# State-space steps over both row halves, with 64-column output tiles and scans of four segments

## The chip, the cores and the metric

The kernel runs on one core of a Trainium2 chip, in one launch. TensorE (PE) multiplies; VectorE (DVE), ScalarE (ACT) and GpSimd (POOL) work on SBUF and PSUM beside it; SyncE (SP) issues the loads. The metric is the device time in microseconds of one execution, median of several runs.

## The reference, cut to what matters

Two residual layers on 256 tokens of 2048 channels, then an RMSNorm. The even layer is the one that the change touches:

```python
proj = rmsnorm(x) @ w_in                     # xa, ga, (u, v), gb: 1024 channels each
a  = exp(lam * dt)                           # complex, 64 groups x 64 states
h[t] = a * h[t-1] + (f * b) @ xa[t]          # per group of 16 channels
y[t] = Re(c @ h[t]) + d_skip * xa[t]
ya = gelu(y);  ya = ya * sigmoid(ya @ w_glu + b_glu) * silu(ga)
yb = gelu(u) * (w_causal @ layernorm(gelu(v)) + b_sp) * silu(gb)
x  = x + concat(ya, yb) @ w_out
```

The odd layer is differential attention with its own projections; the change leaves it alone.

## The kernel before

All large products are made exact to fp32 from float32r operands: a weight is split into a rounded half (wh) and the rest (wl), an activation likewise, and three products are summed. The weights come as a stream of 140 chunks of 1 MB, in the order v, xa, u, gb, ga (w_in, 8 chunks each), eo (the rows of w_out for yb, 8), glu (4), ep (the rows of w_out for ya, 8), then 64 chunks of layer 1's projections and 16 of its output. fetch (line 139) loads a chunk on SP into one of three buffers wr. split (line 156) makes, for each half chunk, wh on ACT (a copy, line 82) and wl on DVE (a subtraction, line 61); wh and wl have three buffers each, so the copy of a half chunk waits until PE has done with the third half before it. gemm_t (line 201) runs 24 matmuls of 512 columns a chunk, gemm_c (line 213) 48 of 256. The results stand in PSUM tiles of tag "m", two of them: v, xa, u, gb and ga have two each, so ga0 takes the place of gb0.

Beside this stream runs side work, written as generators that run_side advances. Of the state-space mixer these are: ssm_params (decays, phases, powers pw of a unit rotation), ssm_consts (line 478: the masked matrices bbr from b, cA and cN from c, and pk, products of both that are added into intra), ssm_bT (line 513: transposes of bbr into bT), e_tables (line 529: E, the rotations of 128 steps, by doubling; one for each half of the channels) and ssm_set (line 558), eight of it. Tokens go in pairs: two inputs enter one step of 128, and two outputs leave it, one by cA and one by cN.

A set S stands for one half of the channels, one of two qh and one half q of the 128 input rows, and covers four channel tiles ct. W (PSUM, one buffer) is 8 matmuls of 64 rows (line 568). On DVE: f, two products of 1024 with E and a sum and difference of 512 that turn W into the rotating frame; eight tensor_tensor_scans of 128 (line 584), each with one decay r2 broadcast along the steps; b, two products back; hst, a sum and a difference, one column to the right of the state before. y (line 594) is four matmuls with intra (line 598) and 16 with cA and cN, tiles of 32 columns, two column groups by turns (line 606). After both q, ACT makes the gelu of y into yaf.

xs (line 679 and after) is xa times the norm's factor, in its token pairs U2 on ACT, 8 copies. After u comes the spatial gate (s, line 700), into ut. After gb, ACT makes gt = silu(gb) in a tile of tag t2, which has three buffers (line 54), DVE multiplies it into ut, and PE transposes ut (ybT, line 722); after ga, at (t2 as well) and its silu.

SP's order is the order of the code. The order on the other engines is made by a scheduler from the code and its priorities; work under hp() goes ahead of what is ready beside it. A tile of a tag takes the buffer that the tile of that tag three (or two, or one) before it in the code had, and its first writer waits for the last reader of that.

Of the kernel before, what the change touches and what calls it, by code (L numbers as in the profile page):

```python
# [10 lines left out]
F32 = mybir.dt.float32  # L11
# [6 lines left out]
T = 256  # L18
# [11 lines left out]
def hybrid_trunk_kernel(ctx: ExitStack, tc: tile.TileContext, xT, xtok, w_in0, w_glu, w_out0,  # L30
# [53 lines left out]
    def rsqrt_mean(name, ss, n, eps, post=None):  # L84
        """(ss / n + eps) ** -0.5: an integer first guess, a cubic step and a Newton step."""
# [32 lines left out]
    # ---------------------------------------------------------------- weight stream  # L118
# [37 lines left out]
    def split(upto, before=None):  # L156
        """hi = the weight rounded to float32r, lo = the exact rest."""
# [80 lines left out]
    # ---------------------------------------------------------------- start: x^T, norm  # L238
# [51 lines left out]
    # the norm's factor: per token on partitions, and as a row on every partition  # L290
# [31 lines left out]
    # ---------------------------------------------------------------- SSM constants  # L322
# [34 lines left out]
    cst = {}  # L357

    def ssm_params():
# [8 lines left out]
        mul(r2, mag, mag)  # L368
# [26 lines left out]
        ep = p32("ep", 64).rearrange("p (c m) -> p c m", c=2)  # L395
# [31 lines left out]
        cst.update(ab=ab, fc=fc, fa=fa, ep=ep)  # L427
        yield
        # powers of exp(i * 2 phi): 1, 2, 4, ..., 64
        pw = []  # L430
        prev = ep
# [31 lines left out]
    def ssm_consts():  # L463
# [34 lines left out]
        # K0 = Re(C bb) and the skip, as one matrix per two pairs  # L498
        intra = cst["intra"]
        pk0 = side1("pk0", [128, 16, 32])  # L500
        for i in range(16):
            for q in range(2):
                P = i * 2 + q
                o = pk0[q * 64:q * 64 + 32, i, :]
                PE.matmul(o, bbr[0][:, P, 1, :], cN[:, 0, P, :], start=True, stop=False)
                PE.matmul(o, bbr[1][:, P, 1, :], cN[:, 1, P, :], start=False, stop=True)
        for q in range(2):
            r = slice(q * 64, q * 64 + 32)
            o = intra[r, :, q * 64:q * 64 + 32]
            add(o, pk0[r], o)  # L510
        yield
# [17 lines left out]
    def e_tables(half):  # L529
# [7 lines left out]
        for k in range(1, 7):  # L537
            n = 1 << k
            for q in range(2):
                ph = slice(q * 8, q * 8 + 8)  # L540
                es = E[:, :, ph, 0:n]
                sh = [128, 8, n]
                m = [t4(f"em{half}{k}{q}{i}", [128, 2, 8, 64])[:, :, :, 0:n] for i in range(2)]
# [12 lines left out]
    hst = sm.tile([128, 2, 4, 129], F32, name="hst", tag="hst")  # L556
    G.memset(hst[:, :, :, 0:1], 0.0)

    def ssm_set(S):
        half, q4 = S // 4, S % 4  # L560
        qh, q = q4 // 2, q4 % 2
        E = etab[half]
        er, ei = (e.rearrange("p (h c q) t -> p h q c t", h=2, q=2)[:, qh, q] for e in (E[:, 0], E[:, 1]))
# [16 lines left out]
        r2 = cst["r2"]  # L580
# [8 lines left out]
        mul(m1, g, erb)  # L589
        mul(m2, g, eib)  # L590
# [4 lines left out]
        if q == 0:  # L595
            ya["y"] = side1(f"y{S}", [128, 4, 128], 1)
            for ct in range(4):
                PE.matmul(ya["y"][:, ct, :], cst["intra"][:, (half * 2 + qh) * 4 + ct, :],
                          U2[:, half, qh, ct, :], start=ct == 0, stop=False, skip_group_check=True)
        y = ya["y"]  # L600
        for ct in range(4):
            P = (half * 2 + qh) * 8 + ct * 2 + q
# [26 lines left out]
    # ---------------------------------------------------------------- layer 0: v, spatial gate  # L629
# [40 lines left out]
    # ---------------------------------------------------------------- layer 0: xa  # L670
# [16 lines left out]
    # ---------------------------------------------------------------- layer 0: u, gb, ga  # L687
# [50 lines left out]
    # ---------------------------------------------------------------- layer 0: output projection  # L738
# [86 lines left out]
    # ---------------------------------------------------------------- layer 1  # L825
# [10 lines left out]
    # lambda  # L836
# [15 lines left out]
    def rope_evac(o, ps, name):  # L852
        """o = the rotated, normalised channels; a map's pairs lie on rows 0-15 and 32-47"""
# [95 lines left out]
            # the second query block meets all keys: its operands in two exact parts  # L949
# [175 lines left out]
```

## Time and profile before

| | us |
|---|---|
| median of 3 runs | 889.18 |
| runs, lowest to highest | 888.95 to 889.61 |
| span of the profiled execution | 887.3 |
| PE busy | 871.7 |
| DVE busy | 666.3 |
| ACT busy | 448.8 |
| PE starts u, gb, ga, eo, glu at | 103.4, 172.9, 223.7, 288.7, 335.0 |

The span runs from the first to the last instruction of the profiled execution; 1.9 us separate it from the median. Busy times overlap. A timeline row of several instructions (x8) gives the first start and the time to the last end; where a row's next start comes before its end, the distance of starts is the slot that the engine gave it.

### The profile page before, as it was taken

To read this page: it belongs to the slowest core of one execution; us is meant where nothing else is said; L and a number is where in the kernel's file an instruction comes from. 1 tells how busy PE (TensorE), PEld (TensorE's weight loads), DVE (VectorE), ACT (ScalarE), POOL (GpSimd) and SP (SyncE) were. 2 spreads that over 40 slices of the span, in tenths; PEclk is the share of its full clock that TensorE was granted. 3 is DMA by queue.
4 is the path that set the end of the run, shared out by engine and by line. 5 is a ranking of instruction groups with operands and counts; after the bars stand their busy time and mean duration, and the time that the engine had idled before them with its cause. 6 is when DMAs were issued, how large, how long until landed. Compare 5 with 4: busy or idle time off the path is not lost.

```text
span 887.3 us, 14016 instructions
## 1 busy us (share of the span) xinstructions
PE 871.7 (98%) x5598; PEld 778.4 (88%) x5598; DVE 666.3 (75%) x1219; ACT 448.8 (51%) x623; POOL 38.3 (4%) x47
## 2 busy tenths in 40 slices
PE   9999999999999999999999999999999999999995
PEld 7799978788999789889988999889988998888895
DVE  8999869999988866567866677666767577665773
ACT  6563862455334645565345543554346544554551
POOL 7110000000000100000000000000000000000000
PEclk9999999999999999999999999999999999999998
DMA  8965452234534655455554545554454455555542
GB/s 306 379 243 191 143 190 96 96 120 166 190 114 141 259 185 176 170 195 202 180 182 160 188 145 190 191 190 152 181 190 171 165 188 196 183 189 190 178 155 96
DMA packets 25985, 160.24 MB, mean 181 GB/s; under 512 B 2880, under 2 KB 4160, under 8 KB 7744
## 3 DMA queue, kind: packets, MB, share of 16 engines
q1 hardware_dynamic: 25344, 156.20, 49.2%
q0 software_dynamic: 576, 3.15, 1.0%
q8 instruction: 44, 0.72, 0.3%
q14 instruction: 21, 0.17, 0.1%
HBM read 157.24 MB, written 2.10 MB: 180 GB/s over the span
## 4 chain that ended last, share of the span: by engine, by line
PE 90%; DVE 7%; ACT 1%; issue 1%; DMA 0%; DVEq 0%; ACTq 0%
PE v L209 5%; PE v L210 5%; PE v L208 5%; PE k L224 3%; PE q L221 3%; PE k L223 3%; PE k L221 3%; PE q L224 3%; PE q L223 3%; PE g L210 3%; PE g L209 3%; PE g L208 3%; PE od L209 2%; PE od L208 2%; PE od L210 2%; PE ga L221 2%
## 5 line engine op out<-in xcount | busy, mean ns | idle before, releaser
L82 ACT ACTIVATE wh<-wr 128x1024 fp32r<-128x1024 f32 (+1 forms) x276 | 288.7, 1047 | 356.0 <-PE v L210 64.0
L61 DVE TENSOR_TENSOR wl<-wr,wh 128x1024 fp32r<-128x1024 f32 (+1 forms) x276 | 331.8, 1205 | 142.2 <-ACT wh L82 141.4
L224 PE MATMUL k<-h2h,wl 128*128 128x256 f32 x256 | 72.8, 284 | 0.0
L221 PE MATMUL q<-h2h,wh 128*128 128x256 f32 x256 | 72.7, 284 | 0.0
L223 PE MATMUL q<-h2l,wh 128*128 128x256 f32 x256 | 72.7, 284 | 0.0
L224 PE MATMUL q<-h2h,wl 128*128 128x256 f32 x256 | 72.6, 284 | 0.0
L221 PE MATMUL k<-h2h,wh 128*128 128x256 f32 x256 | 72.4, 283 | 0.0
L223 PE MATMUL k<-h2l,wh 128*128 128x256 f32 x256 | 72.4, 283 | 0.0
L209 PE MATMUL v<-wl,h2h 128*128 128x512 f32 x128 | 50.8, 397 | 0.0
L209 PE MATMUL g<-wl,h2h 128*128 128x512 f32 x128 | 50.3, 393 | 0.0
L210 PE MATMUL g<-wh,h2l 128*128 128x512 f32 x128 | 50.1, 391 | 0.0
L210 PE MATMUL v<-wh,h2l 128*128 128x512 f32 x128 | 50.0, 390 | 0.0
L208 PE MATMUL v<-wh,h2h 128*128 128x512 f32 x128 | 50.0, 390 | 0.0
L208 PE MATMUL g<-wh,h2h 128*128 128x512 f32 x128 | 49.9, 390 | 0.0
L224 PEld LDWEIGHTS k<-h2h,wl 128*128 128x128 f32 x256 | 49.1, 192 | 0.1
L221 PEld LDWEIGHTS q<-h2h,wh 128*128 128x128 f32 x256 | 49.1, 192 | 0.2
L221 PEld LDWEIGHTS k<-h2h,wh 128*128 128x128 f32 x256 | 49.1, 192 | 0.0
L223 PEld LDWEIGHTS k<-h2l,wh 128*128 128x128 f32 x256 | 49.1, 192 | 0.0
L223 PEld LDWEIGHTS q<-h2l,wh 128*128 128x128 f32 x256 | 49.1, 192 | 0.0
L224 PEld LDWEIGHTS q<-h2h,wl 128*128 128x128 f32 x256 | 49.1, 192 | 0.0
L209 PE MATMUL od<-wl,oh 128*128 128x512 f32 x96 | 37.6, 392 | 0.0
L208 PE MATMUL od<-wh,oh 128*128 128x512 f32 x96 | 37.5, 391 | 0.0
(331 smaller groups left out, 2182.8 us busy)
## 6 DMA issues: line engine op xcount, KB each, us to landing
wr<-in_w_in_dram SPq DMA_DIRECT2D x100, 1024.0 KB, 4.8
wr<-in_w_out_dram SPq DMA_DIRECT2D x32, 1024.0 KB, 4.8
wr<-in_w_glu_dram SPq DMA_DIRECT2D x4, 1024.0 KB, 4.7
wr<-in_w_in_dram SPq DMA_DIRECT2D x8, 256.0 KB, 4.5
wr<-in_w_in_dram SPq DMA_DIRECT2D x4, 512.0 KB, 7.9
xk<-in_xtok_dram SPq DMA_DIRECT2D x2, 1024.0 KB, 10.9
xr<-in_xtok_dram POOLq DMA_DIRECT2D x2, 1024.0 KB, 7.6
out_dram<-x SPq DMA_DIRECT2D x6, 256.0 KB, 2.6
```

The source lines that it names most:

```text
L61: (eng or V).tensor_tensor(out=o, in0=a, in1=b, op=op)
L82: A.activation(out=o, in_=i, func=f, **kw)
L208: PE.matmul(ps[:, t, :], hi[:, s], wh, start=first and a == 0, stop=False)
L209: PE.matmul(ps[:, t, :], hi[:, s], wl, start=False, stop=False)
L210: PE.matmul(ps[:, t, :], lo[:, s], wh, start=False, stop=last and a == len(ktiles) - 1)
L221: PE.matmul(ps[:, c, :], wh[:, s], hi, start=first and a == 0 and c % 2 == 0, stop=False, skip_group_check=True)
L223: PE.matmul(ps[:, c, :], wh[:, s], lo, start=False, stop=False, skip_group_check=True)
L224: PE.matmul(ps[:, c, :], wl[:, s], hi, start=False, stop=fin, skip_group_check=True)
```

## The change

A set S now covers both row halves q and two channel tiles a. W has a place for each q in a bank of its own, and its 8 matmuls go by turns to rows 0 to 63 and 64 to 127. The eight scans become two of 512, over four segments of 128 in a row; a tile R holds the decay of each segment with a zero at each segment's first column, which cuts the carry. R is a t2 tile: POOL clears column 0, ACT copies the broadcast r2 into the rest. hst loses its extra column and is written shifted. y is made per set: two matmuls with intra and eight with cc, 64-column tiles that hold Ca and Ca^2 side by side, both times from the same columns of hst; the second output of a step now takes its own input's and its fellow's share from intra. For that ssm_params makes a2 = a^2, ssm_consts a fourth set of masked products, and pk 128 matmuls (64 of 32 and 64 of 64 columns) where it had 64, in two halves. yaf takes 32 smaller gelus for 16. The E table's doubling works on 2 x w x n elements at once, 28 operations a half for 72, on the same elements; pw and r2 are kept in the order of the steps.

```diff
 # ssm_consts
+                ("ab", c_re, c_im, cc[0][:, :, 0, :], cc[1][:, :, 0, :], -1.0),
+                ("a2", c_re, c_im, cc[0][:, :, 1, :], cc[1][:, :, 1, :], -1.0)):
...
+            for w in range(2):
+                for i in range(8):
+                    for q in range(2):
+                        lhs = [z[:, P].rearrange("p j h -> p (j h)") if w else z[:, P, 1, :] for z in bbr]
+                        o = pk0[q * 64:q * 64 + (64 if w else 32), i, w, :]
+                        PE.matmul(o, lhs[0], cN[:, 0, P, :], start=True, stop=False, skip_group_check=True)
+                        PE.matmul(o, lhs[1], cN[:, 1, P, :], start=False, stop=True, skip_group_check=True)
 # e_tables
-                for i in range(2):
-                    a = pw[k][:, i, half * 16 + q * 8:half * 16 + q * 8 + 8].unsqueeze(2).to_broadcast(sh)
-                    for c in range(2):
-                        mul(m[i][:, c], es[:, c], a)
+                for i in range(2):
+                    a = pw[k][:, i, half * 16 + ph.start:half * 16 + ph.stop]
+                    mul(m[i], es, a.unsqueeze(1).unsqueeze(3).to_broadcast([128, 2, w, n]))
 # ssm_set
-        rows = slice(q * 64, q * 64 + 64)
-        W = side2(f"W{S}", [128, 2, 4, 128])
+        W = side2(f"W{S}", [128, 2, 2, 2, 128])
         for c in range(2):
-            for ct in range(4):
-                PE.matmul(W[:, c, ct, :], cst["bT"][c][rows, (half * 2 + qh) * 4 + ct, :],
-                          U2[rows, half, qh, ct, :], start=True, stop=True)
+            for a in range(2):
+                for q in range(2):
+                    rows = slice(q * 64, q * 64 + 64)
+                    ct = cp * 2 + a
+                    PE.matmul(W[:, q, c, a, :], cst["bT"][c][rows, (half * 2 + qh) * 4 + ct, :],
+                              U2[rows, half, qh, ct, :], start=True, stop=True)
+        R = t2(f"R{S}", [128, 4, 128])
+        G.memset(R[:, :, 0:1], 0.0)
+        act(R[:, :, 1:128], cst["r2"][:, P:P + 4].unsqueeze(2).to_broadcast([128, 4, 127]), AF.Copy)
...
-            for ct in range(4):
-                P = (half * 2 + qh) * 8 + ct * 2 + q
-                V.tensor_tensor_scan(out=g[:, c, ct, :], data0=r2[:, P:P + 1].to_broadcast([128, 128]),
-                                     data1=g[:, c, ct, :], initial=0.0, op0=ALU.mult, op1=ALU.add)
+            gf = g[:, c].rearrange("p s t -> p (s t)")
+            V.tensor_tensor_scan(out=gf, data0=R.rearrange("p s t -> p (s t)"), data1=gf, initial=0.0,
+                                 op0=ALU.mult, op1=ALU.add)
...
-        sub(h[:, 0, :, 1:129], m1[:, 0], m2[:, 1])
-        add(h[:, 1, :, 1:129], m1[:, 1], m2[:, 0])
+        sub(h[:, 0, :, 1:128], m1[:, 0, :, 0:127], m2[:, 1, :, 0:127])
+        add(h[:, 1, :, 1:128], m1[:, 1, :, 0:127], m2[:, 0, :, 0:127])
...
-            for i, cm in ((0, cst["cA"]), (1, cst["cN"])):
-                o = y[q * 64 + i * 32:q * 64 + i * 32 + 32, ct, :]
-                for c in range(2):
-                    PE.matmul(o, cm[:, c, P, :], h[:, c, ct, i:i + 128], start=False, stop=c == 1,
-                              skip_group_check=True)
+        for a in range(2):
+            for c in range(2):
+                for q in range(2):
+                    PE.matmul(y[q * 64:q * 64 + 64, a, :], cst["cc"][c][:, P + a * 2 + q].rearrange("p i h -> p (i h)"),
+                              h[:, c, q * 2 + a, :], start=False, stop=c == 1, skip_group_check=True)
```

How this moves the instructions at the end of gb. On ACT, before, around the first silu of gb (gt00, gt01 are those of gb0; wh28 to wh30 are copies of chunks of gb):

```order
L82 ACTIVATE wh28_0_2439<-wr28_2369 128x1024
L82 ACTIVATE yaf_1372<-y2_1406 32x512 x4
L82 ACTIVATE wh28_1_2443<-wr28_2369 128x1024
L82 ACT_TABLE_LOAD
L82 ACTIVATE gt00_2471<-gb0_2334,rs0_187 128x512
L82 ACTIVATE wh29_0_2494<-wr29_2403 128x1024
L82 ACTIVATE gt01_2474<-gb0_2334,rs0_187 128x512
L82 ACTIVATE wh29_1_2498<-wr29_2403 128x1024
L82 ACTIVATE wh30_0_2528<-wr30_2437 128x1024
```

and after (R7 is the decay row of set 7, y4 the output of set 4, wh32 and wh33 copies of chunks of ga):

```order
L82 ACTIVATE wh33_0_2568<-wr33_2476 128x1024
L82 ACTIVATE R7_1901<-r2_278 128x4x127
L82 ACTIVATE yaf_1352<-y4_1795 32x256 x4
L82 ACT_TABLE_LOAD
L82 ACTIVATE gt00_2387<-gb0_2250,rs0_187 128x512
L82 ACTIVATE gt01_2390<-gb0_2250,rs0_187 128x512
L82 ACTIVATE gt10_2544<-gb1_2407,rs0_187 128x512
L82 ACTIVATE gt11_2547<-gb1_2407,rs0_187 128x512
L82 ACTIVATE yh1_2248<-ybT0_2393 128x512
L82 ACT_TABLE_LOAD
```

The silus of gb0 stood among the copies of gb's own chunks; now all four stand in a row behind R7 and the gelu of y4.

On PE, before, at the last half chunk of gb (gb1) and the first matmuls of ga0:

```order
L208 MATMUL gb1_2491<-wh31_1_2566,hh1_153 128x512
L221 MATMUL ga0_2649<-hh0_152,wh32_0_2596 128x256
L223 MATMUL ga0_2649<-hl0_154,wh32_0_2596 128x256
L209 MATMUL gb1_2491<-wl31_1_2567,hh1_153 128x512
L210 MATMUL gb1_2491<-wh31_1_2566,hl1_155 128x512
L208 MATMUL gb1_2491<-wh31_1_2566,hh1_153 128x512
```

and after:

```order
L210 MATMUL gb1_2407<-wh31_1_2482,hl1_155 128x512
L600 MATMUL W5_1810<-U2_208,bT0_1022 128x128 x4
L600 MATMUL W5_1810<-U2_208,bT1_1023 128x128 x4
L637 MATMUL y4_1795<-hst_209,cc0_603 64x128 x2
L637 MATMUL y4_1795<-hst_209,cc1_604 64x128 x2
L637 MATMUL y4_1795<-hst_209,cc0_603 64x128 x2
L637 MATMUL y4_1795<-hst_209,cc1_604 64x128 x2
L600 MATMUL W6_1851<-U2_208,bT0_1022 128x128 x4
L600 MATMUL W6_1851<-U2_208,bT1_1023 128x128 x4
L632 MATMUL y5_1836<-U2_208,intra_582 128x128 x2
L753 MATMUL ybT0_2393<-ident_132,ut_1933 128x128
L637 MATMUL y5_1836<-hst_209,cc0_603 64x128 x2
L221 MATMUL ga0_2565<-hh0_152,wh32_0_2512 128x256
L223 MATMUL ga0_2565<-hl0_154,wh32_0_2512 128x256
```

ga0 followed gb1 directly, even ahead of its last matmuls; now W5, the products of y4, W6 and the beginnings of y5 and ybT0 stand between.

On DVE, before, at the product of ut with gt00:

```order
L61 TENSOR_TENSOR em1410_1779<-E1_1719,pw4_382 128x8x16 x2
L61 TENSOR_TENSOR ut_2017<-ut_2017,gt00_2471 128x512
L61 TENSOR_TENSOR E1_1719<-em1400_1771,em1401_1772 128x8x16 x2
L61 TENSOR_TENSOR wl29_0_2495<-wr29_2403,wh29_0_2494 128x1024
L61 TENSOR_TENSOR ut_2017<-ut_2017,gt01_2474 128x512
L61 TENSOR_TENSOR em1411_1780<-E1_1719,pw4_382 128x8x16 x2
```

and after:

```order
L61 TENSOR_TENSOR wl33_0_2569<-wr33_2476,wh33_0_2568 128x1024
L61 TENSOR_TENSOR b14_1789<-f14_1781,E1_1723 128x1024
L61 TENSOR_TENSOR b24_1790<-f14_1781,E1_1723 128x1024
L61 TENSOR_TENSOR hst_209<-b14_1789,b24_1790 128x4x127 x2
L61 TENSOR_TENSOR f15_1822<-W5_1810,E1_1723 128x1024
L61 TENSOR_TENSOR f25_1823<-W5_1810,E1_1723 128x1024
L61 TENSOR_TENSOR f15_1822<-f15_1822,f25_1823 128x512 x2
L618 SCALAR_TENSOR_TENSOR f15_1822<-R5_1819,f15_1822 128x512 x2
L61 TENSOR_TENSOR b15_1830<-f15_1822,E1_1723 128x1024
L61 TENSOR_TENSOR b25_1831<-f15_1822,E1_1723 128x1024
L61 TENSOR_TENSOR ut_1933<-ut_1933,gt00_2387 128x512
L61 TENSOR_TENSOR hst_209<-b15_1830,b25_1831 128x4x127 x2
L61 TENSOR_TENSOR f16_1863<-W6_1851,E1_1723 128x1024
```

That product stood within the building of E1, ahead of set 4; now it stands in set 5, between b and hst.

## Rows read from the trace of the kernel before

**Rows 1.** The page: busy time, share of the span and instructions of each engine; the granted clock of PE in tenths of full speed, in 40 slices; the chain that ended last, by engine.

```profile
PE 871.7 (98%) x5598; PEld 778.4 (88%) x5598; DVE 666.3 (75%) x1219; ACT 448.8 (51%) x623; POOL 38.3 (4%) x47
...
PEclk9999999999999999999999999999999999999998
...
PE 90%; DVE 7%; ACT 1%; issue 1%; DMA 0%; DVEq 0%; ACTq 0%
```

**Rows 2.** The table by stage: stretch, its length, busy time of PE, PEld, DVE, ACT and POOL (instructions), granted clock, DMA share, GB/s.

```profile
0.00:133.00 133.00, 128.61 (x869) 113.20 (x870) 116.45 (x342) 84.88 (x116) 24.54 (x28) 1.00 0.67 242
133.00:226.60 93.60, 91.73 (x553) 76.39 (x553) 89.34 (x181) 40.90 (x49) 0.00 (x0) 1.00 0.35 124
226.60:288.70 62.10, 62.10 (x543) 59.10 (x543) 55.89 (x77) 24.89 (x28) 0.00 (x0) 1.00 0.41 144
288.70:335.00 46.30, 45.94 (x226) 37.54 (x225) 33.09 (x35) 26.93 (x31) 4.10 (x7) 1.00 0.58 216
335.00:887.00 552.00, 543.30 (x3415) 492.20 (x3413) 371.58 (x585) 271.22 (x399) 9.68 (x12) 0.99 0.50 176
```

**Rows 3.** PE's timeline, the rows of u and gb with an idle time: start, us, what, and in brackets the idle time before and its releaser.

```profile
113.06 0.50 PE L209 MATMUL u<-wl,hh 128*128 128x512 f32 x1 [0.77 <-DVE wl L61]
...
131.26 0.66 PE L521 MATMUL pbt<-ident,bbr 128*128 128x128 f32 x4 [0.76 <-ACT bT L82]
...
134.94 0.50 PE L208 MATMUL u<-wh,hh 128*128 128x512 f32 x1 [0.46 <-ACT ut L82]
...
172.94 0.50 PE L208 MATMUL gb<-wh,hh 128*128 128x512 f32 x1 [1.41 <-ACT ut L82]
```

**Rows 4.** PE's timeline at the change from gb to ga, and the first rows of eo and glu.

```profile
223.23 0.39 PE L210 MATMUL gb<-wh,hl 128*128 128x512 f32 x1
223.45 0.39 PE L208 MATMUL gb<-wh,hh 128*128 128x512 f32 x1
223.68 0.28 PE L221 MATMUL ga<-hh,wh 128*128 128x256 f32 x1
...
226.43 0.28 PE L224 MATMUL ga<-hh,wl 128*128 128x256 f32 x1
226.55 0.28 PE L221 MATMUL ga<-hh,wh 128*128 128x256 f32 x1
...
288.66 0.40 PE L208 MATMUL eo<-wh,yh 128*128 128x512 f32 x1
...
335.01 0.28 PE L221 MATMUL glu<-yah,wh 128*128 128x256 f32 x1
```

**Rows 5.** PE's timeline: W of a set and the row after it, and matmuls of y with cA and cN.

```profile
131.85 1.16 PE L568 MATMUL W<-U,bT 64*128 64x128 f32 x8
132.93 0.66 PE L521 MATMUL pbt<-ident,bbr 128*128 128x128 f32 x4
...
180.05 0.27 PE L606 MATMUL y<-hst,cA 128*32 128x128 f32 x1
180.06 0.27 PE L606 MATMUL y<-hst,cN 128*32 128x128 f32 x1
180.16 0.27 PE L606 MATMUL y<-hst,cA 128*32 128x128 f32 x1
```

**Rows 6.** The matmuls of pk, by tile: duration in ns as minimum, median, maximum; first and last start in us; form.

```profile
L505 PE MATMUL pk<-cN,bbr x64: 196/196/217, 90.4 to 99.0; 128*32 128x32 f32 x64
L506 PE MATMUL pk<-cN,bbr x64: 196/196/217, 97.0 to 99.1; 128*32 128x32 f32 x64
```

**Rows 7.** DVE's timeline: the first f; the scans and b of set 1, hst, and the first f of set 2; the row of E1's building with an idle time.

```profile
133.04 2.36 DVE L61 TENSOR_TENSOR f<-W,E 128x1024 f32<-128x1024 f32 x2 [1.06 <-PE W L568]
...
151.45 2.63 DVE L584 TENSOR_TENSOR_SCAN f<-r,f 128x128 f32<-128x128 f32 x8
154.12 2.36 DVE L61 TENSOR_TENSOR b<-f,E 128x1024 f32<-128x1024 f32 x2
156.39 1.22 DVE L61 TENSOR_TENSOR wl<-wr,wh 128x1024 fp32r<-128x1024 f32 x1
157.53 1.29 DVE L61 TENSOR_TENSOR hst<-b,b 128x512 f32<-128x512 f32 x2
158.73 2.35 DVE L61 TENSOR_TENSOR f<-W,E 128x1024 f32<-128x1024 f32 x2
...
194.56 0.19 DVE L61 TENSOR_TENSOR em<-E,pw 128x32 f32<-128x32 f32 x1 [1.10 <-ACT U L82]
```

**Rows 8.** ACT's timeline: the first U copies and three silus of gb (gt).

```profile
105.36 5.30 ACT L82 ACTIVATE U<-xs 32x512 f32<-32x512 f32 x8
...
202.91 0.69 ACT L82 ACTIVATE gt<-gb,rs 128x512 f32<-128x512 f32 x1 [0.59 <-PE gb L210]
...
226.63 0.69 ACT L82 ACTIVATE gt<-gb,rs 128x512 f32<-128x512 f32 x1 [1.92 <-PE gb L210]
...
228.17 0.68 ACT L82 ACTIVATE gt<-gb,rs 128x512 f32<-128x512 f32 x1
```

**Rows 9.** DVE's timeline: the scans of set 4 and the row after them, and the scans of set 7.

```profile
238.11 2.62 DVE L584 TENSOR_TENSOR_SCAN f<-r,f 128x128 f32<-128x128 f32 x8
240.65 1.20 DVE L61 TENSOR_TENSOR wl<-wr,wh 128x1024 fp32r<-128x1024 f32 x1
...
291.08 2.62 DVE L584 TENSOR_TENSOR_SCAN f<-r,f 128x128 f32<-128x128 f32 x8
```

More of the change, by code (lines that the diff above doesn't have):

```diff
@@ L357, in hybrid_trunk_kernel, with pairs, step_order @@
     cst = {}
+    def pairs(z):
+        return z.rearrange("p (g a q) -> p g a q", a=2, q=2)
+    def step_order(z):
+        return z.rearrange("p (g q a) -> p g a q", a=2, q=2)
     def ssm_params():
@@ L367, in ssm_params @@
         r2 = p32("r2")
-        mul(r2, mag, mag)
+        mul(step_order(r2), pairs(mag), pairs(mag))
         cst["r2"] = r2
@@ L426, in ssm_params @@
         add(fa[:, 1, :], t1, t2_)
-        cst.update(ab=ab, fc=fc, fa=fa, ep=ep)
+        a2 = p32("a2", 64).rearrange("p (c m) -> p c m", c=2)
+        mul(t1, ab[:, 0, :], ab[:, 0, :])
+        mul(t2_, ab[:, 1, :], ab[:, 1, :])
+        sub(a2[:, 0, :], t1, t2_)
+        stt(a2[:, 1, :], ab[:, 0, :], 2.0, ab[:, 1, :], ALU.mult, ALU.mult)
+        cst.update(ab=ab, a2=a2, fc=fc, fa=fa, ep=ep)
         yield
         pw = []
-        prev = ep
+        prev_ = p32("eps", 64)
+        V.tensor_copy(out=step_order(prev_), in_=pairs(ep_))
+        prev = prev_.rearrange("p (c m) -> p c m", c=2)
         for j in range(7):
@@ L499, in ssm_consts @@
         intra = cst["intra"]
-        pk0 = side1("pk0", [128, 16, 32])
-        for i in range(16):
-            for q in range(2):
[L503 to L511, printed above, removed]
+        for hf in range(2):
+            pk0 = side1(f"pk0{hf}", [128, 8, 2, 32], hf)
+            for w in range(2):
+                for i in range(8):
+                    for q in range(2):
+                        P = (hf * 8 + i) * 2 + q
+                        lhs = [z[:, P].rearrange("p j h -> p (j h)") if w else z[:, P, 1, :] for z in bbr]
+                        o = pk0[q * 64:q * 64 + (64 if w else 32), i, w, :]
+                        PE.matmul(o, lhs[0], cN[:, 0, P, :], start=True, stop=False, skip_group_check=True)
+                        PE.matmul(o, lhs[1], cN[:, 1, P, :], start=False, stop=True, skip_group_check=True)
+            for q in range(2):
+                hs = slice(hf * 8, hf * 8 + 8)
+                for r, cols, src in ((slice(q * 64, q * 64 + 32), slice(q * 64, q * 64 + 32), 0),
+                                     (slice(q * 64, q * 64 + 64), slice(q * 64 + 32, q * 64 + 64), 1)):
+                    o = intra[r, hs, cols]
+                    add(o, pk0[r, :, src, :], o)
+            yield
     def ssm_bT():
@@ L588, in ssm_set @@
         m2 = t4(f"b2{S}", [128, 2, 4, 128])
-        mul(m1, g, erb)
-        mul(m2, g, eib)
+        mul(by_q(m1), by_q(g), er)
+        mul(by_q(m2), by_q(g), ei)
         h = hst
-        sub(h[:, 0, :, 1:129], m1[:, 0], m2[:, 1])
-        add(h[:, 1, :, 1:129], m1[:, 1], m2[:, 0])
+        sub(h[:, 0, :, 1:128], m1[:, 0, :, 0:127], m2[:, 1, :, 0:127])
+        add(h[:, 1, :, 1:128], m1[:, 1, :, 0:127], m2[:, 0, :, 0:127])
         yield
[L595 to L599, printed above, removed]
@@ new lines, in ssm_set @@
+        for a in range(2):
+            ct = cp * 2 + a
+            PE.matmul(y[:, a, :], cst["intra"][:, (half * 2 + qh) * 4 + ct, :], U2[:, half, qh, ct, :],
+                      start=a == 0, stop=False, skip_group_check=True)
+        for a in range(2):
+            for c in range(2):
+                for q in range(2):
+                    PE.matmul(y[q * 64:q * 64 + 64, a, :], cst["cc"][c][:, P + a * 2 + q].rearrange("p i h -> p (i h)"),
+                              h[:, c, q * 2 + a, :], start=False, stop=c == 1, skip_group_check=True)
@@ L617, in ssm_set @@
+        yield
+        if "f" not in ya:
+            ya["f"] = t8(7, "yaf", [128, 8, T])
+        for q in range(2):
+            for i in range(2):
+                r = slice((qh * 2 + q) * 32, (qh * 2 + q) * 32 + 32)
+                cs = half * 4 + cp * 2
+                o = ya["f"][r, cs:cs + 2, :].rearrange("p c (t i) -> p c i t", i=2)[:, :, i, :]
+                act(o, y[q * 64 + i * 32:q * 64 + i * 32 + 32], AF.Gelu_apprx_tanh)
         yield
```

48 lines of the change are left out of this document (20 added, 28 removed).

## The prediction

> **What bounds the kernel now.** I read the page first, for the engine that never rests: TensorE (PE) is busy in 871.7 of 887.3 us, its granted clock is at full speed (2.4 GHz, tenths of 9) through the whole span, and 90% of the chain that ended last is PE [rows 1]. So the time is PE's list of matmuls plus the gaps in it. Then the table by stage [rows 2]: I cut the span at the start of u's state-space work (133), of ga (226.6), of eo (288.7) and of glu (335.0). VectorE (DVE) is the near second only between 133 and 226.6, with 89.3 of 93.6 us; there it does the weights' low halves and the state-space steps together. Then PE's own timeline, for rows with an idle time: in u and gb these are 0.77, 0.76, 0.46 and 1.41 us, 3.4 us in all [rows 3]. All else that the change can save on PE is matmul work, not waiting.
>
> **What the weight products cost.** A 128x512 matmul starts every 0.227 us (two slots in 0.45), so a chunk of 24 takes 5.44 us; a 128x256 one every 0.12 us, so ga's 384 take 46.1 us [rows 4]. Neither changes.
>
> **PE's side work.** Before, W of one set is 8 matmuls that leave 16 records, 8 in 1.08 us where one follows the other; with the switches of tile shape, about 2.0 us a set. The y products with cA and cN run side by side on two column groups (starts 0.01 us apart, pairs every 0.11 us), about 1.9 us a set [rows 5]. After, W alternates row halves 0 to 63 and 64 to 127. No row of before shows two row halves at once: the price is between 2.0 us (one after the other) and 1.0 us (side by side as the column groups are). I take 1.0, since the column groups' rows are the nearest case of two tiles. The Trainium skill (TensorEngine Tiling (Array Packing), Key Properties) says that different tiles can load weights and multiply in parallel; by that rule W costs the 1.0 us, and if it failed for row halves the sum would be the serial rival's below. The 64-column y tiles halve the streams: 8 pairs of records for 16, about 1.0 us a set for 1.9. pk goes from 64 to 128 matmuls; before they took 2.3 us, their starts from 97.0 to 99.1 but for two early ones [rows 6]. Alternating 32- and 64-column tiles, I put it at 6.0, with 4.1 (twice the work at its present pairs) and 9 (no pair side by side) as ends. So PE loses, over eight sets, 8 us of W and 7 to 8 of y, gains 3.7 of pk, and some of the 3.4 us of gaps go: a gain of 12 to 15 us **if nothing new waits**. That sum is a rival, not my forecast.
>
> **DVE's side work.** Two products of 1024 take 2.27 us, the two of hst 1.20 [rows 7]: slots of 1.133 and 0.60, so 1.04 ns an element plus 0.067 us. Eight scans of 128 take 2.54 us, 0.318 each [rows 9]. For a scan of 512 the rows give ends of 1.27 (four of the old) and 0.60 (a product of 512); with the product's fixed part taken off, 0.318 means about two slots an element, hence 1.12, which I take. A set (f 2.27 and 1.20, scans, b 2.27, hst 1.20) then falls from 9.48 to 9.18 us. The E table keeps its elements and drops 44 operations a half: 44 x 0.067 = 2.9 us. These are small beside 89.3. The a2 products add six operations of 512, 3.6 us, ahead of u, where E0 gives 2.9 back and DVE has 116.5 us in 133.0 [rows 2]; what is left is counted in the delay of u below.
>
> **At nothing.** POOL's memsets: it is busy 38.3 us in all [rows 1]. ACT's eight R copies (0.6 each, as the silus of 512 are [rows 8]), four more masked copies and 16 more gelus of half the size: ACT has 40.9 us of 93.6 in the stage [rows 2], so their time is hidden, their place in ACT's order is not.
>
> **The new wait.** The order of after is what counts. R0 to R7, the scans' decay rows, come out of the three t2 buffers that gt also uses, and all eight stand in the program ahead of gt00. The first Silu evacuation of gb, gt00, therefore takes the buffer of R5 and can't start until set 5's scans have read it. On ACT gt00 to gt11 stand behind R7, which waits for set 4's scans, and behind y4's gelu. ga0 takes the PSUM of gb0, which gt01 empties, and gt01 waits until DVE has multiplied gt00 into ut. So PE, at the end of gb, has only W5, y4, W6 and part of y5 to do until DVE is through set 5. Before, gt00 waited for nothing but its own PSUM, and gt10 and gt11 ran at 226.63 and 228.17 while ga was under way; sets 4 to 7 were spread over gb, ga and eo, with scans from 238.11 to 291.08 [rows 8, 9].
>
> **When does ga0 start?** By DVE's queue. Its first f comes at 133.04 before, after waiting for W0 [rows 7]. After, u begins about 4.2 us later (pk, and a second half-chunk held behind the U copies, whose row is 5.30 us [rows 8]), less 1.0 for W0 and the 0.76 and 0.46 of gaps: 135.5. From there to the product with gt00 DVE has, by its order, five sets whole and the sixth up to hst (55.0 - 1.2), 24 low halves (27.2), four groups of ut (4.1), xs1 (1.1), E1 (14.6) and that product (0.6): 101.4 us. Two things add: about 1.8 us where the low half of chunk 27 waits for its copy behind eight U copies (before, the like wait was 1.10 [rows 7]), and 0.65 for slots between operations (by the same sum before's stretch comes out 1.3% short; half of that). Then gt01, 0.69 on ACT, and two hand-overs, 0.85 together. ga0 starts at 135.5 + 101.4 + 2.45 + 0.85 = **240.2**, where before it started at 226.4 in earnest [rows 4].
>
> By a second road, a floor: the copies of chunk 33's first half need a weight buffer that the last half of gb frees. From gb's end it is one copy (1.05), its low half (1.13), b and hst of set 4 (3.5), f and scans of set 5 (5.7), b of set 5 (2.3), the product and gt01 (1.4): 15.1 us whatever DVE did before. With gb ending at 221.0 to 223.4 (226.4, plus pk and the later waits, less five W, four y and the gaps) ga0 can't start before 236.1 to 238.5. The two roads agree within 4 us; DVE's queue is the longer.
>
> **From ga0 on.** PE has 46.1 us of ga and 8.5 of side work left (the rest of y5, W7, y6, y7, the 15 other transposes): eo starts at 240.2 + 54.6 = 294.8 against 288.66. DVE reaches chunk 33's second half and chunk 34 barely in time (within 0.5 us by the same slots), so 0 to 1.5 us may come on top. eo then has no state-space work left in it: 43.5 us for 46.3 [rows 2, 4]. glu starts at 338.3 against 335.0, **3.3 us late**. Past glu the order has the same work, and the other 552 us stay. Span 890.6; the profiled span is 1.9 us under the median of 889.18 (888.95 to 889.61), so **892.5 us**. What this kernel's measurement can tell from no change is about 0.2%, or 1.8 us.
>
> **Rivals.**
> *The buffer wait costs little (faster).* If DVE were some 15 us ahead at the end of gb, set 5 would be through and PE would keep most of the 12 to 15 us: 874 to 877. For it: after removes about 2.4 + 2.9 us of DVE work and DVE had some idle slots. Against it: DVE is 95% full in that stage [rows 2] and the floor above doesn't move with its lead, since the copies of chunk 33 start only when gb ends. Chance 0.07.
> *Cheaper pieces (same to faster).* Scans at 0.60, pk at 4.1 and no copy wait bring DVE's queue down to the floor; set 5's two scans take 1.0 off that as well: ga0 at 235.1 to 237.5, glu 1.8 us early to 0.6 late, 887.4 to 889.8. If gb ends at 220 as well, 886. Chance 0.33, of which 0.20 within 0.2% and 0.13 below it.
> *Row halves one after the other (slower).* W costs 1.0 us more where it stands in DVE's or PE's way, at W0 and W7 (W5 and W6 lie in PE's wait): 2 x 1.0, 894.5. For it: no row shows row halves together. Decides from the first W on: whether the two halves' records start together. Chance 0.12.
> *DVE falls further behind.* pk at 9, and stalls at chunks 33 to 35: 2 to 4 us more, 894 to 897. It is the forecast's upper end.
>
> **How the numbers follow.** The forecast has 0.48, its late end (DVE further behind) with it; 0.46 of that lies over 0.2% slower and 0.02 within. With the serial rival's 0.12 slower has 0.58; within 0.2% has 0.22 (0.20 and 0.02); faster 0.20 (0.13 and 0.07). The range reaches from 885.0 (cheap scans, cheap pk, gb early) to 897.0 (dear pk and stalls in ga) and leaves out the 874 to 877 of the first rival and the far tail of the last.
>
> **What would show it.** Right: in PE's timeline one idle time of 9 to 13 us, cut by W5, y4, W6 and y5, between the last gb matmul (near 222) and the first of ga (near 240), released by ACT's gt; gt00 starting right after set 5's second scan; eo free of y; each scan row near 1.1 us; W records of the two halves starting together. Wrong: ga0 following gb at once; scans near 0.6 us; DVE idle by more than 5 us between 136 and 236; or a gap of similar size elsewhere, such as at u, where pk and the copies stand.

## The result, and the profile after

| | before | after | forecast |
|---|---|---|---|
| median, us | 889.07 (888.59 to 889.61, 4 runs) | 900.0 (899.29 to 901.02, 4 runs) | 892.5 (885.0 to 897.0) |
| ratio to before | 1 | 1.012 (1.0106 to 1.0135) | 1.004 |
| profiled span, us | 887.3 | 899.3 | 890.6 |

The changed kernel is slower, as forecast, but by 10.9 us instead of 3.4, and the time lies outside the range. The profile is of the longest of the four runs, 901.02 us: by its span it is 8.7 us above the forecast, where the median is 7.5 above. The page of after, the lines of [rows 1]:

```profile
PE 869.1 (97%) x5598; PEld 774.6 (86%) x5598; DVE 666.4 (74%) x1100; ACT 458.0 (51%) x650; POOL 38.4 (4%) x56
...
PEclk9999999999799999999999999999999999999998
...
PE 83%; DVE 11%; issue 2%; ACT 2%; DMA 1%; SPq 0%; DVEq 0%; ACTq 0%
```

PE has 2.6 us less busy time and 12 us more span; DVE's share of the chain that ended last rose from 7% to 11%, and the granted clock has a dip that before's hasn't. The stages tell where: glu starts at 346.96 against 335.01, 11.95 late, and from there on the two kernels run alike. So I read PE's timeline up to glu for waits (start, us, what, idle before and releaser):

```profile
62.32 0.39 PE L224 MATMUL xa<-hh,wl 128*128 128x256 f32 x1 [1.74 <-DVE wl L61]
62.54 0.28 PE L221 MATMUL xa<-hh,wh 128*128 128x256 f32 x1
...
63.80 0.42 PE L223 MATMUL xa<-hl,wh 128*128 128x256 f32 x1
64.01 0.41 PE L224 MATMUL xa<-hh,wl 128*128 128x256 f32 x1
...
178.32 0.79 PE L208 MATMUL gb<-wh,hh 128*128 128x512 f32 x1 [4.67 <-ACT ut L82]
178.91 0.63 PE L209 MATMUL gb<-wl,hh 128*128 128x512 f32 x1
...
229.65 0.39 PE L210 MATMUL gb<-wh,hl 128*128 128x512 f32 x1
229.97 1.16 PE L600 MATMUL W<-U,bT 64*128 64x128 f32 x16
236.26 2.15 PE L637 MATMUL y<-hst,cc 128*64 128x128 f32 x16 [5.12 <-DVE hst L61]
239.22 2.08 PE L600 MATMUL W<-U,bT 64*128 64x128 f32 x16 [0.81 <-DVE f L61]
241.22 1.22 PE L632 MATMUL y<-U,intra 128*128 128x128 f32 x4
245.70 0.48 PE L753 MATMUL ybT<-ident,ut 128*128 128x128 f32 x1 [3.25 <-DVE ut L61]
246.30 0.69 PE L637 MATMUL y<-hst,cc 128*64 128x128 f32 x4
246.92 0.58 PE L221 MATMUL ga<-hh,wh 128*128 128x256 f32 x1
247.30 0.41 PE L223 MATMUL ga<-hl,wh 128*128 128x256 f32 x1
```

Four things are to be seen. At 62.32, in xa, PE waits 1.74 us for a low half, and a little later the 128x256 matmuls come every 0.21 us instead of 0.12. At 178.32, ahead of gb0, it waits 4.67 us for the evacuation of u1, with slow matmuls behind it again. From 229.97, the end of gb, to 246.92, the first matmul of ga, it has only two W, y4 and the beginnings of y5 and ybT0, and waits 5.12, 0.81 and 3.25 us, for hst, f and the product with gt00. And behind that gap the matmuls of ga start at 0.21 us once more. The table by stretch gives the granted clock of these places (length, then busy us of PE, PEld, DVE, ACT and POOL, the clock, DMA share, GB/s):

```profile
60.00:70.00 10.00, 8.26 (x56) 8.06 (x56) 9.87 (x14) 2.63 (x3) 0.00 (x0) 0.83 0.41 141
172.00:185.00 13.00, 8.33 (x36) 6.56 (x34) 12.86 (x17) 4.58 (x7) 0.10 (x1) 0.74 0.23 82
246.00:256.00 10.00, 9.88 (x69) 8.39 (x69) 10.00 (x14) 5.10 (x9) 0.00 (x0) 0.73 0.00 0
```

DVE around the first f and at the end of the gap, where [rows 7] had 133.04 for the first f:

```profile
139.74 1.23 DVE L61 TENSOR_TENSOR wl<-wr,wh 128x1024 fp32r<-128x1024 f32 x1 [1.50 <-ACT wh L82]
140.89 2.35 DVE L61 TENSOR_TENSOR f<-W,E 128x1024 f32<-128x1024 f32 x2
...
240.31 2.33 DVE L618 TENSOR_TENSOR_SCAN f<-R,f 128x512 f32<-128x512 f32 x2
242.68 2.36 DVE L61 TENSOR_TENSOR b<-f,E 128x1024 f32<-128x1024 f32 x2
244.96 0.68 DVE L61 TENSOR_TENSOR ut<-ut,gt 128x512 f32<-128x512 f32 x1
245.56 1.28 DVE L61 TENSOR_TENSOR hst<-b,b 128x508 f32<-128x508 f32 x2
```

And ACT, where [rows 8] had gt00 at 202.91 (R is the decay row of a set):

```profile
175.41 0.62 ACT L82 ACTIVATE R<-r 128x508 f32<-128x508 f32 x1 [2.72 <-DVE f L618]
176.06 0.69 ACT L82 ACTIVATE ut<-u,rs 128x512 f32<-128x512 f32 x1
...
238.45 1.61 ACT L82 ACTIVATE yaf<-y 32x256 f32<-32x256 f32 x4 [5.64 <-PE y L637]
242.72 1.28 ACT L82 ACT_TABLE_LOAD   x1 [2.66 <-DVE f L618]
244.02 0.69 ACT L82 ACTIVATE gt<-gb,rs 128x512 f32<-128x512 f32 x1
245.68 0.69 ACT L82 ACTIVATE gt<-gb,rs 128x512 f32<-128x512 f32 x1 [0.97 <-DVE ut L61]
```

gt00 starts 1.4 us behind the end of set 5's scans (240.31 + 2.33), after a table load of 1.28, as its wait on R5's buffer has it; gt01 ends at 246.37 and ga0 follows. At 175.41 the copy of R5, which waits for set 2's scans, stands ahead of u1's evacuation (ut): that is the wait ahead of gb0.

### The profile page after: what moved, and what is told of

Read it like the earlier page. It is cut to its first block, busy times and chain, and to the rows that moved or that the text cites. A ratio compares the mean times of both kernels' runs of the same rounds, so it can differ in the third digit from the quotient of the medians.

```text
span 899.3 us, 13960 instructions
## 1 busy us (share of the span) xinstructions
PE 869.1 (97%) x5598; PEld 774.6 (86%) x5598; DVE 666.4 (74%) x1100; ACT 458.0 (51%) x650; POOL 38.4 (4%) x56
## 4 chain that ended last, share of the span: by engine, by line
PE 83%; DVE 11%; issue 2%; ACT 2%; DMA 1%; SPq 0%; DVEq 0%; ACTq 0%
PE v L209 4%; PE v L210 4%; PE v L208 4%; PE k L224 3%; PE q L221 3%; PE k L221 3%; PE k L223 3%; PE q L224 3%; PE q L223 3%; PE g L210 3%; PE g L209 3%; PE g L208 3%; DVE wl L61 3%; PE od L208 2%; PE od L209 2%; PE od L210 2%
## 5 line engine op out<-in xcount | busy, mean ns | idle before, releaser
L224 PE MATMUL xa<-hh,wl 128*128 128x256 f32 x128 | 37.0, 291 | 1.7 <-DVE wl L61 1.7
L221 PE MATMUL ga<-hh,wh 128*128 128x256 f32 x128 | 37.7, 294 | 0.0
```

The lines of the kernel that those rows point to most:

```text
L221: PE.matmul(ps[:, c, :], wh[:, s], hi, start=first and a == 0 and c % 2 == 0, stop=False, skip_group_check=True)
L224: PE.matmul(ps[:, c, :], wl[:, s], hi, start=False, stop=fin, skip_group_check=True)
```

## The experiments

Medians of the timed runs, with the ratio to the kernel before on the same chip and its 95% interval:

| run | what it is | us | ratio |
|---|---|---|---|
| after | the change | 900.0 | 1.012 (1.0106 to 1.0135) |
| e1 | after, gt in PSUM | 888.25 | 0.9991 (0.998 to 1.0001) |
| e2 | before, gt in PSUM | 889.13 | 1.0 (0.9991 to 1.001) |
| e3 | before, scans of 512 | 901.67 | 1.0139 (1.0122 to 1.0156) |
| e4 | after, old E | 902.8 | 1.015 (1.0135 to 1.0165) |
| e5 | after, scans of 128, no R | 887.34 | 0.9966 (0.995 to 0.9982) |
| e6 | e1, R copied by POOL | 894.08 | 1.0048 (1.0027 to 1.0068) |
| e7 | e5, E in products of 512 | 883.16 | 0.9928 (0.9913 to 0.9943) |
| e8 | before, wide E | 891.92 | 1.0028 (1.0019 to 1.0038) |
| e9 | after, E in products of 512 | 908.38 | 1.0214 (1.0197 to 1.0231) |
| e10 | e7, W by row half | 887.23 | 0.9975 (0.9966 to 0.9984) |
| e11 | after, scans of 128, old E | 883.59 | 0.993 (0.9913 to 0.9947) |
| e12 | e3, gt in PSUM | 886.14 | 0.9961 (0.9946 to 0.9976) |
| e13 | e1, old E | 886.65 | 0.9972 (0.9961 to 0.9984) |

**The shared buffers.** e1 takes gt out of t2, e2 is its control:

```diff
-                gt = t2(f"gt{n}{t}", [128, 512])
+                gt = ps[:, t, :]
                 act(gt, ps[:, t, :], AF.Silu, scale=rsx[0][:, t:t + 1])
```

> The changed kernel, with silu of gb written in place into gb's PSUM tile, so that it takes no t2 buffer; R0 to R7 keep theirs. Theory A (the shared t2 buffers make the gap ahead of ga): ga0 follows gb within 1 us, the 17.0 us between them shrink to under 1, the clock loss of about 1.5 us behind the gap goes too; sets 5 to 7 spread over ga and eo again. About 11 us less than the changed kernel's 900: 887 to 891. Theory B (the state-space queue of DVE is the bound, the buffer only shows where): PE waits as long at other places of gb and ga, 897 to 900.

> The kernel before with the same silu in place in PSUM: a control for the edit of e1. gt took its t2 buffer at once in the kernel before, so nothing waits less; gb's PSUM is held until DVE has multiplied, 0.6 to 1.3 us longer per tile. Both theories: 888.5 to 891.

e1 gains 11.75 us on after, e2 is level with before. PE's timeline of e1, ahead of gb0 and at the first matmul of ga:

```profile
178.22 0.80 PE L208 MATMUL gb<-wh,hh 128*128 128x512 f32 x1 [4.65 <-ACT ut L82]
...
228.74 0.28 PE L221 MATMUL ga<-hh,wh 128*128 128x256 f32 x1
```

ga0 now has no idle time before it and starts 18.2 us earlier; the wait ahead of gb0 is untouched. At glu (334.45) 12.5 of the 18.2 us are left, since the state-space work that stood in the gap now lies in ga and eo. Theory A holds for the gap, theory B falls. e3 is the other side, one part of the change put into the kernel before:

```diff
+        R = t2(f"R{S}", [128, 4, 128])
+        G.memset(R[:, :, 0:1], 0.0)
+        rq = cst["r2"].rearrange("p (s t q) -> p s t q", t=4, q=2)[:, half * 2 + qh, :, q]
+        act(R[:, :, 1:128], rq.unsqueeze(2).to_broadcast([128, 4, 127]), AF.Copy)
...
-            for ct in range(4):
-                V.tensor_tensor_scan(out=g[:, c, ct, :], data0=r2[:, P:P + 1].to_broadcast([128, 128]), ...)
+            V.tensor_tensor_scan(out=gf, data0=R.rearrange("p s t -> p (s t)"), data1=gf, ...)
```

> The kernel before with only the scans changed: two scans of 512 with a decay row R in t2, made on ACT, for eight of 128; W, y, pk and E as before. Theory A: the gap ahead of ga appears by this alone, 12 to 18 us between gb and ga0, and the time goes to 897 to 903. Theory B (it is W, y, pk and the sets over both row halves that fill DVE's and PE's order): no gap, 887 to 890, since the scans save 0.3 us a set. It also shows whether the early wait at 62 us (xa, 1.74 us) comes with the R copies on ACT (then it is here) or with the wide E operations (then it isn't).

The scans alone bring the gap, with every set, W, y and pk as before. PE's timeline of e3 between gb and ga0 (243.9):

```profile
225.66 3.28 PE L568 MATMUL W<-U,bT 64*128 64x128 f32 x16 [1.87 <-DVE f L61]
233.28 1.03 PE L608 MATMUL y<-hst,cA 128*32 128x128 f32 x3 [4.34 <-DVE hst L61]
...
242.72 0.33 PE L724 MATMUL ybT<-ident,ut 128*128 128x128 f32 x1 [3.70 <-DVE ut L61]
```

And e12 takes only the sharing out of e3 again (the edit of e1):

> e3 (the kernel before with only the scans of 512) with gt in PSUM, so that R shares t2 with nothing of gb. Theory A: e3's 12 us over the kernel before are the shared buffer and nothing else: 887 to 891, no gap ahead of ga. If the scans of 512 or the R copies cost something of their own, 892 to 897.

15.5 us less than e3 and 0.4% less than before: the scans of 512 are worth some 3.5 us by themselves, and the shared buffer turned that into a loss of 12. In e3 there is no idle time in xa, so the R copies on ACT alone don't make the early wait; nor is there one of note ahead of gb0 in e12 (0.30 us), although R5's copy stands ahead of u1's evacuation there too. The order alone doesn't make that wait: set 2's scans have to be late as well.

**No R at all.** e5 puts the eight scans of 128 back into after and drops R:

```diff
-        R = t2(f"R{S}", [128, 4, 128])
...
+            for s in range(4):
+                V.tensor_tensor_scan(out=g[:, c, s, :], data0=cst["r2"][:, P + s:P + s + 1].to_broadcast([128, 128]),
+                                     data1=g[:, c, s, :], initial=0.0, op0=ALU.mult, op1=ALU.add)
```

> The changed kernel with the old eight scans of 128 a set, so that there is no R at all: sets, W, y, pk and E stay as changed, gt stays in t2. Theory A (R in t2 makes both late waits: gt00 behind set 5, and the evacuation of u1 on ACT behind the copy of R5, which waits for set 2's scans): the gap ahead of ga and 3.3 of the 4.7 us ahead of gb0 go, with the slow clock behind both (1.5 and 2.0 us); DVE pays 0.3 us a set more. 900 less 16 to 18, plus up to 2: 882 to 886. Theory B (the wait ahead of gb0 comes from the sets' own order): it stays, and the time is that of e1, 888 to 890.

Both late waits shrink as theory A has it; PE's row of gb0 in e5:

```profile
176.91 0.50 PE L208 MATMUL gb<-wh,hh 128*128 128x512 f32 x1 [1.52 <-ACT ut L82]
```

The time, 887.34 (882.93 to 889.76 over 10 runs), misses the expected 882 to 886. In the profiled run PE waits elsewhere: 2.26 us in v, with slow matmuls behind it, 2.33 within pk, and 2.11 at 212.20, in gb. The loss in v isn't made by the edit's order: at the first matmul of xa e5 is 3.3 us behind e7 (below), which up to 59 us has the same order on every engine and waits 1.55 us there. What else makes it no run here shows; the runs of e5 alone lie 6.8 us apart.

**R on POOL.** e6 is e1 with one engine changed:

```diff
-        act(R[:, :, 1:128], cst["r2"][:, P:P + 4].unsqueeze(2).to_broadcast([128, 4, 127]), AF.Copy)
+        G.tensor_copy(out=R[:, :, 1:128], in_=cst["r2"][:, P:P + 4].unsqueeze(2).to_broadcast([128, 4, 127]))
```

> e1 with the copies into R on POOL, so that ACT has none of them; the scans of 512 and R in t2 stay. Theory A: u1's evacuation no longer stands behind R5, the wait ahead of gb0 falls from 4.65 us to about 1.4, the slow clock behind it goes: e1's 888.25 less 4 to 5, 883 to 885. Theory B: the wait stays, 887 to 889. POOL's copies could slow DVE beside them; that would show as longer DVE rows and take back 1 to 2 us.

The wait ahead of gb0 falls, from 4.65 to 2.30 us, so R5's place on ACT made about half of it, as far as two traces of different order tell; but the time rises by 5.8 us, against both theories. Part of it can be read: three of POOL's copies of R, and DVE's products of b beside the first two of them:

```profile
151.57 3.69 POOL L605 COPY R<-r 128x508 f32<-128x508 f32 x1
...
166.31 1.56 POOL L605 COPY R<-r 128x508 f32<-128x508 f32 x1
...
192.78 0.61 POOL L605 COPY R<-r 128x508 f32<-128x508 f32 x1
```

```profile
152.44 2.35 DVE L61 TENSOR_TENSOR b<-f,E 128x1024 f32<-128x1024 f32 x2
...
166.18 2.77 DVE L61 TENSOR_TENSOR b<-f,E 128x1024 f32<-128x1024 f32 x2
```

A copy takes 0.61 us where it is quick and 3.69 in the first of these rows, with DVE at work all along; the pair of b beside the next copy takes 2.77 for 2.35. The Trainium skill (SBUF — State Buffer, SBUF: two separate sides) says that a VectorE instruction with two inputs in SBUF and a GpSimd one that reads SBUF want the same pair of ports, and that the one that starts first holds it while the other waits. These rows agree: copy or product gets longer. That is 0.4 us a copy, and not 5.8. Half of the 5.8 stands elsewhere: at the first matmul of xa (57.16 against 54.27) e6 is 2.9 us behind e1, after a wait of 2.35 us in v like that of e5, which has no R. Later come 2.28 us within pk (e5: 2.33) and waits for low halves in gb (3.13 us at 197.09, 2.27 at 220.06), where the order had changed. So e6 gives no price for R on POOL.

**The early wait.** In after, DVE at 61:

```profile
59.91 1.22 DVE L61 TENSOR_TENSOR em<-E,pw 128x1024 f32<-128x1024 f32 x1
61.04 1.22 DVE L61 TENSOR_TENSOR wl<-wr,wh 128x1024 fp32r<-128x1024 f32 x1
```

The low half for which PE waits until 62.32 stands behind a product of 1024 of E's building. e4 takes the wide operations out of after, e8 puts them alone into before:

> The changed kernel with the old building of the E table (72 operations a half). If the wide operations, 1.13 us each ahead of a low half, make the wait of 1.74 us at 62 and the slow clock behind it, xa gains 3.2 us and E1 costs 2.9 more ahead of the gap: 899 to 901. If the R copies on ACT make that wait, it stays and the E operations come on top: 902 to 904.

> The kernel before with only the E table in the wide operations. If these by themselves make the early wait, it appears near 61 us with a slow clock behind it, and the time is 889 to 892 (3 us lost in xa, 2.9 of DVE won in gb that PE can use only where it waits for DVE); if the wait needs the other parts (R copies, the third cleared matrix) as well, none appears and the time is 887.5 to 889.5.

PE's row in e4, and then in e8:

```profile
61.60 0.39 PE L224 MATMUL xa<-hh,wl 128*128 128x256 f32 x1 [0.61 <-DVE wl L61]
```

```profile
62.16 0.38 PE L224 MATMUL xa<-hh,wl 128*128 128x256 f32 x1 [1.60 <-DVE wl L61]
```

The wide operations by themselves make the wait (e8, 1.60 us, though with no slow clock behind it); without them it falls from 1.74 to 0.61 and no slow clock follows. e8 is 0.3% slower although DVE has 44 operations a half less, but that is not the price of this wait alone, for PE has a second new wait there, in u:

```profile
140.60 1.16 PE L698 MATMUL s<-vt,bw 128*128 128x128 f32 x8 [1.94 <-DVE ut L79]
```

In e4 the first f came 2.2 us earlier than in after, and yet ga0 came 3.0 us later (249.92). From the first f to the end of the product with gt00 DVE took 5.2 us longer: 3.4 for the old building of E1, and 1.8 more of idle time, most of it ahead of a low half that waits for its copy, which waits for gb's late and slow matmuls. DVE's rows:

```profile
138.66 1.23 DVE L61 TENSOR_TENSOR f<-W,E 128x1024 f32<-128x1024 f32 x1 [0.63 <-PE W L602]
...
184.27 1.23 DVE L61 TENSOR_TENSOR wl<-wr,wh 128x1024 fp32r<-128x1024 f32 x1 [2.09 <-ACT wh L82]
```

Hence 902.8: neither outcome expected of e4 came alone, and what was won ahead of the first f was mostly lost again before ga0.

e7 and e9 build E in products of 512 (w = min(16, 256 // n)), e7 on top of e5 and e9 on top of after:

> e5 with the E table built in operations of at most 512 elements a product instead of 1024. If the 1024-wide products ahead of a low half make the wait at 62 us with the slow clock behind it (1.74 and 1.47 us), it goes or falls below 0.8: e5 less 2 to 3 us. If it stays, e5 plus 0 to 0.5 us for the added operations.

> The changed kernel with the E table in products of at most 512 elements and nothing else undone: R, its t2 buffers and both late waits stay. Theory C (the step of the prediction that failed is the start of the first f, 5.4 us too early, and most of that is the early wait in xa with the slow clock behind it): the wait at 62 us goes, xa6 starts about 4 us earlier, the first f and ga0 come 3 to 4 us earlier (12 more operations a half cost 0.8), and the time is 896 to 897.5. Theory D (whatever is won early is lost in the waits ahead of gb0 and ga0, since DVE's queue is full): ga0 and the time move by less than 1 us, 899 to 901.

e7 gains 4.2 us on e5 and is the fastest kernel of the study, with e11. But it is no test of the early wait: e5's trace has no idle time in xa to begin with, and of the 5.3 us between the two traces 3.3 are there at the first matmul of xa, where the order is still the same. e9 loses 8.4 us, and both theories fall: a wait in xa stayed (1.20 us at 63.97), and others are longer. PE's timeline of e9, in v and in u:

```profile
43.77 0.50 PE L209 MATMUL v<-wl,hh 128*128 128x512 f32 x1 [1.99 <-DVE wl L61]
...
121.54 0.49 PE L208 MATMUL u<-wh,hh 128*128 128x512 f32 x1 [2.51 <-ACT wh L82]
```

With them the first f of e9 came at 146.27:

```profile
146.27 2.35 DVE L61 TENSOR_TENSOR f<-W,E 128x1024 f32<-128x1024 f32 x2
```

That is 5.4 us later than in after; ga0 came 7.3 later and the median 8.4. Of the 5.4, 2.2 were lost by the first matmul of xa, where e9 still has after's order on every engine, so the smaller products didn't make that part. What is lost ahead of the first f isn't absorbed by the later waits here, it moves them: theory D falls by the opposite sign. The reverse isn't shown, as e4 has it. Why e9 has those two gaps and e7 hasn't I haven't settled.

**PE's side work.** e10 orders W's matmuls by row half:

```diff
-        for c in range(2):
-            for a in range(2):
-                for q in range(2):
+        for q in range(2):
+            for c in range(2):
+                for a in range(2):
```

> e7 with W's eight matmuls ordered by row half (four on rows 0 to 63, then four on 64 to 127) instead of by turns. If the turns are what lets the two halves run at once, W's 16 records of a set take 1.8 to 2.0 us instead of 1.1, and over eight sets PE loses up to 7 us where it is the bound: 886 to 890. If the gain of W is hidden in waits anyway, 883 to 885.

W of one set in e10, and then in e7:

```profile
200.25 1.71 PE L600 MATMUL W<-U,bT 64*128 64x128 f32 x16
```

```profile
197.01 1.16 PE L600 MATMUL W<-U,bT 64*128 64x128 f32 x16
```

16 records in 1.71 us by halves, in 1.16 by turns: the turns are what lets the two halves run at once. Eight times 0.55 is 4.4, and the time rose by 4.1, but that the two agree is in part luck: 1.6 us of the difference are there at the first matmul of xa, ahead of the first W, where the order is the same. e11 leaves only the sets, the 64-column outputs, a2 and pk:

> The changed kernel with both the old scans (no R) and the old building of E: what is left of the change is the sets over both row halves, the 64-column outputs, a2 and pk. If these are worth what PE's side work says once nothing new waits, 877 to 883; if the longer pk and the constants ahead of u take it back, 884 to 889.

883.59, 0.7% less than before, just above the first range. Summed over all records of e11's trace (each to the next start, idle time left out), W falls from 16.4 to 10.6 us, y from 20.7 to 12.3, and pk rises from 2.3 to 6.9: 9.6 us less work, 6.1 of which reach the time.

**What holds e1 back.** e13 is e1 with the old E:

> e1 with the old building of E as well: sets over both halves, scans of 512 with R in t2, gt in PSUM. If the wide E operations are what keeps e1 at 888 (early wait and slow clock, 3.2 us), 880 to 885, near e11. If it is R's place on ACT ahead of the evacuation of u1 (wait ahead of gb0 with the slow clock behind it), that wait of 3 to 5 us stays and the time is 885 to 889; both may show, each by its own row.

1.6 us less than e1, with the early wait at 0.61: the first theory holds in part. Ahead of gb0 3.19 us are still there, but not for the second theory's reason. PE has products of y ahead of gb0, and they wait for hst, while ACT was through with u1's evacuation at 175.53:

```profile
175.81 1.08 PE L639 MATMUL y<-hst,cc 128*64 128x128 f32 x6 [3.19 <-DVE hst L61]
```

## Why the prediction was wrong, step by step

The mechanism was right: the gap ahead of ga, its cause (gt00 behind set 5's scans through R's buffers) and its length, 16.95 us (9.3 of them idle), where the floor gave 15.1 and DVE's queue 16.8 or more. e1, e3 and e12 show the cause from three sides. So were the scan of 512 (slots of 1.13 us for 1.12, rows of 1.21 each), the two row halves at once (16 records of W in 1.16 us), and eo without y: 43.55 us for 43.5. The Trainium skill (TensorEngine Tiling (Array Packing), Key Properties) has the rule that different tiles can work in parallel; W's rows and e10 bear it out.

**The step that failed** is "135.5", the start of the first f. It came at 140.89. The sum's terms against the trace of after:

| term | forecast | measured | off by |
|---|---|---|---|
| first f | 135.5 | 140.89 | +5.4 |
| from there to the end of the product with gt00 | 103.85 | 104.7 | +0.8 |
| gt01 and hand-overs to ga0 | 0.85 | 1.36 | +0.5 |
| ga0 to eo0 | 54.6 | 56.5 | +1.9 |
| eo | 43.5 | 43.55 | 0 |
| sum (span) | 890.6 | 899.3 | +8.7 |

The table is of the profiled run; by the medians the sum is 7.5 us off.

The 5.4 us: I took xa as unchanged, and xa6 (the first matmul of xa's chunk 6) started 4.45 us late, from 0.55 at xa0, the wait of 1.74, the slow clock behind it (1.47, the excess of those matmuls over 0.12 us each) and some 0.7 in the rows around that wait and the first matmuls of pk. e8 shows the wide E as able to make such a wait by itself, e4 that it makes most of this one. I had booked E's wider operations as a gain of 2.9 us of DVE and never asked what waits behind one of them; they stand ahead of low halves that PE is about to need. From xa6 to u2 the forecast 4.2 us were right (4.2), though not by pk as I put it: pk took 6.9 us for 6.0. My terms (133.04 and 4.2, less 1.0, 0.76 and 0.46) add up to 135.0, not 135.5, so 0.5 of what was missing was in by a slip. And of the credit of 2.2 us (W0, and two of PE's gaps) 0.8 came: the first f stands behind a low half in DVE's queue (139.74, itself waiting for its copy), so an earlier W0 buys nothing. In e9 a later start of the first f goes through to the end (5.4 later there, 8.4 in the time); in e4 an earlier one didn't (of 2.2 us DVE lost 1.8 again). So how much of the 8.7 us an early first f alone would have saved stays open.

**The second road** went wrong by more: gb ended at 229.97, not at 221.0 to 223.4, after the waits in xa and ahead of gb0 and the slow matmuls behind both. ACT's copy of chunk 33's first half, and DVE's low half of it:

```profile
230.08 1.06 ACT L82 ACTIVATE wh<-wr 128x1024 fp32r<-128x1024 f32 x1 [1.66 <-PE gb L210]
```

```profile
232.01 1.21 DVE L61 TENSOR_TENSOR wl<-wr,wh 128x1024 fp32r<-128x1024 f32 x1
```

The copy was done at 231.14, 0.87 us before DVE came to it. DVE's queue was the longer road, as forecast, but by this little: a shorter queue with the same end of gb would have gained about 0.9 us (an estimate from these two rows).

**The clock** was in no term: the 1.9 us from ga0 to eo0 are 1.5 of slow matmuls behind the gap, and 1.5 of the early 4.45 are the same. I priced waits at their length, and they cost more.

**The wait ahead of gb0** (4.67 us and 2.0 of slow clock) I did not forecast either. In after it lies just within what DVE's queue takes anyway: that took 104.7 us from the first f to the product, where the sum has 103.85, and stood idle for 1.4 of them. In e1, where the gap is gone, it is PE's longest wait; its price there no run shows by itself, since e6, which halved it, lost time elsewhere.

**The rivals.** That the buffer wait costs little didn't happen, and without that wait (e1) the kernel is level with before, not at 874 to 877: PE's work falls by 9.6 us, not by 12 to 15 with the gaps, and e1 gives nearly all of it back: ahead of glu its PE is idle for 12.2 us where before's is for 6.6, and the slow matmuls in xa and gb cost 3.5. Scans at 0.60 and row halves in turn did not happen. DVE falling further behind, which I kept within the forecast's late end, is nearest to what came, but by waits ahead of u and not by stalls in ga.

## What to carry to other kernels

A new temporary in a rotating buffer puts its reader ahead of every later user of that buffer; look up who takes it next, in code order, and what that instruction stands in front of. A wider operation saves its fixed cost and holds its queue for longer: ask which short, urgent work stands behind it. And a kernel at 98% PE can pay for a wait of some microseconds twice, by the wait and by slow matmuls behind it. Last, two traces can differ before the edit has touched anything: compare them at a place ahead of it first, and count only what comes on top.

## What I had not expected of the hardware

Behind the wait of 1.74 us in xa the matmuls ran at half rate (0.21 us for 0.12, the lower of the two clock levels, 1.2 GHz) from 63.6 to 67.0, a granted clock of 0.83 over that stretch of 10 us; behind 4.67 us in gb 0.74, behind the gap 0.73. In xa the slow rows begin 1.3 us after the wait has ended, behind the gap at once. Before's wait of 1.41 us [rows 3], e8's of 1.60 and e7's of 1.86 ahead of gb0 had no slow rows behind them, nor had e6's of 2.30 there; those of 2.26 (e5) and 1.99 (e9) in v had. What tells these apart no run here settles.
